# An output projection as seven block products instead of eight, in a one-core hybrid encoder layer

## The chip, the cores and the metric

The kernel runs on one core of a Trainium2 chip. The metric is the device time of one execution in microseconds. A profiled execution also gives a span, from its first to its last instruction. The engines are TensorE (PE in the profile), VectorE (DVE), ScalarE (ACT), GpSimd (POOL) and SyncE (SP), whose queue issues the transfers here.

## The reference

Sequence length and model width are 1024, one layer. Everything is float32.

```python
h = layer_norm(x, emb_ln_g, emb_ln_b)
proj = h @ w_in                      # q k v z_a u z_b g_a g_b
y_a = neighbourhood_attention(q, k, v, rpb) * silu(z_a)      # 8 heads x 64
u = centred_depthwise_conv(u, conv_w, conv_b)
y_b = (rg_lru(u, forward) + rg_lru(u, backward)) * silu(z_b)
m = sigmoid(g_a + b_merge[0]) * (y_a @ w_ba) + sigmoid(g_b + b_merge[1]) * (y_b @ w_bb)
out = m @ w_out
return layer_norm(ALPHA * h + out, ln_g, ln_b)
```

The change concerns the last three lines: the merged branches `m` (1024 tokens by 1024 channels), the product `m @ w_out` with a 1024 by 1024 weight, and the closing layer norm.

## The kernel before

**Products in three passes.** An operand is split into a high part, its cast to the matmul's fp32r type, and a low part, the remainder (`lo_of`, line 127: a subtraction on VectorE or GpSimd). `mm3` (line 130) multiplies high by high, low by high and high by low, so each block of 128 rows of the contraction costs three matmuls.

**The stages.** A first layer norm, the input projection, the convolution and the recurrences, then the second branch's product together with the attention, then the first branch's product with the merge, then the output projection. VectorE, ScalarE, GpSimd and SyncE follow the order in which the code is written (`manual_schedule`), and so does TensorE: each engine's queue is in order, and an instruction that waits holds up what is behind it on its engine. Across engines only data and buffers order the work.

**The input projection** already uses seven block products instead of eight (`OPS`, line 145; s1 to s4 are sums of weight blocks, T1 to T4 sums of the activations). This scheme is Winograd's form of Strassen's product for a 2 by 2 split of both operands: four sums on each operand, seven products, and sums of the results.

**The branch slots** (line 1316): 16 slots, two for each of the eight channel blocks `j`, one for each half `n` of the tokens. In a slot TensorE makes `mb`, twelve matmuls of 512 columns, in a PSUM bank. VectorE multiplies by the gate (`b_gate`, line 1013) and adds the second branch's part `m` (`merge`, line 1300), ScalarE casts to the high part `mh`, VectorE subtracts for the low part `ml`. Beside that ScalarE and GpSimd split the next branch weight (`b_split`) and one row block of the output weight, `wo`, 128 by 1024, in two slots.

**The output projection** (line 1390): for each of eight token tiles `i` two halves of 512 columns (the last tile's second half in two pieces of 256), each 24 matmuls into one bank (`o_product`). VectorE adds the scaled residual `z` (loaded from `h_d`) and takes statistics. Then `newton` makes the reciprocal root, ScalarE scales the row, GpSimd multiplies by the gain and adds the bias (`gb2`), SyncE stores it. The last tile is finished by VectorE alone, in four pieces. Banks are taken in turn from the tags mb, s and tp, two banks each; the banks of `acc` stay unused here.

Of the kernel before, what the change touches and what calls it, by code (L numbers as in the profile page):

```python
# [10 lines left out]
F32 = mybir.dt.float32  # L11
F32R = mybir.dt.float32r
# [55 lines left out]
def encoder_kernel(ctx, tc, x, gb1, gb, w_qk, w_v, w_s, w_ba, w_bb, w_gate, smalls, bias, w_out, out):  # L68
# [58 lines left out]
    def lo_of(eng, lo, full, hi):  # L127
        eng.tensor_tensor(lo, full, hi.bitcast(F32), ALU.subtract)  # L128
# [10 lines left out]
    def run(gen):  # L139
        for _ in gen:  # L140
            pass
# [865 lines left out]

    def b_group(which, j, n, y, o, ks=range(4)):

        yield from mm3(o[:], [([t[:, k, :] for t in b_w[which, j]], [t[:, k, halves[n]] for t in y]) for k in ks],  # L1010
                       quantum=1, first=ks[0] == 0, last=ks[-1] == 3)

    def b_gate(which, j, n, o):
# [61 lines left out]

    yb = late["yb"]
    yap = pool("yap")
    ya = pair(yap, [P, 4, S], "ya")
    at0 = pool("at0")
    acc = [pst.tile([P, HALF], F32, name=f"acc{g}") for g in range(2)]  # L1080
# [103 lines left out]

    def gated(h, n):
        hp = h // 2
        at_, (hi, lo) = attns[hp][:, halves[n]], [t[:, hp, halves[n]] for t in ya]
        G.tensor_tensor(at_, at_, gates[hp][:, halves[n]], ALU.mult)
        G.tensor_copy(hi, at_)
        lo_of(G, lo, at_, hi)  # L1190

    def last_half(g):

        h, hp = H - 1, H // 2 - 1

        def product(n):
            at_ = attns[hp][:, halves[n]]
            V.tensor_tensor(at_, at_, gates[hp][:, halves[n]], ALU.mult)
            A.copy(ya[0][:, hp, halves[n]], at_)

        def low(n):
            lo_of(V, ya[1][:, hp, halves[n]], attns[hp][:, halves[n]], ya[0][:, hp, halves[n]])
# [23 lines left out]
    for unit in range(-NT, H * NT + PV_LAG):  # L1226
# [50 lines left out]
        if unit == H * NT:  # L1277

            for pl in (late["hd"], late["hd0"], late["ybp"]):
                pl.release()  # L1280
            wop = pool("wop", "right")
            wo = [pair(wop, [P, D], f"wo{k}") for k in range(NK - 2)]
            wos = {}

            def w_load(k):
                if k < NK:
                    wos[k] = wop.tile([P, D], F32, tag="wos", bufs=3, name=f"wos{k}")
                    SP.dma_start(wos[k][:], w_out[k * P:(k + 1) * P, :])
# [4 lines left out]
            for k in range(3):  # L1293
                w_load(k)
    assert filled == sum(FILL)


    sums_m, mh, ml = {}, {}, {}

    def merge(j, n, o):  # L1300
        b_gate(0, j, n, o)
        V.tensor_tensor(o[:], o[:], late["m", j, n][:], ALU.add)
        mh[j, n] = late["mp"].tile([P, HALF], F32R, tag=f"m{j}{n}", name=f"mh{j}{n}")
        A.copy(mh[j, n][:], o[:])

    def merge_lo(j, n, o):
        lo_of(V, ml[j, n][:], o[:], mh[j, n][:])
# [6 lines left out]
    banks[0] = pst  # L1314
    turns.append(itertools.chain(["mb", "mb", "s"], itertools.cycle(["tp", "mb", "s"])))
    for slot in range(2 * NK + 2):
        j, n = divmod(slot, 2)
        if 2 < slot <= 2 * NK:
            merge(*divmod(slot - 1, 2), sums_m[slot - 1])
        if slot == 2:  # L1320
            at0.release()
            mlp = pool("mlp")
            ml.update({(j, n): mlp.tile([P, HALF], F32R, name=f"ml{j}{n}") for j in range(NK) for n in range(2)})
            wo += [pair(mlp, [P, D], f"wo{k}") for k in range(NK - 2, NK)]
            merge_lo(0, 0, sums_m.pop(0))
        for q in (1,) if slot == 3 else (slot - 2,) if slot > 3 else ():
            merge_lo(*divmod(q, 2), sums_m.pop(q))
        if j < NK:
            if n == 0:
                b_load(0, j + 2)  # L1330
            g_load(0, j + 1, n, **(dict(tag=f"u{slot % 4}", bufs=1) if slot % 4 else dict(tag="z", bufs=5)))
            o = sums_m[slot] = bank(f"mb{j}{n}")

            run(b_group(0, j, n, ya, o, range(3 if slot < 2 else 4)))
            if 0 < slot < 3:
                run(b_group(0, 0, slot - 1, ya, sums_m[slot - 1], range(3, 4)))
            if n == 0 and j > 0:
                b_split(0, j + 1, A)
            if 0 < slot < 3:
                merge(0, slot - 1, sums_m[slot - 1])  # L1340

        if slot % 2:
            if j < NK:
                A.copy(wo[j][0][:], wos[j][:])
            if j > 0:
                w_load(j + 2)
        elif slot > 0:
            lo_of(G, wo[j - 1][1][:], wos.pop(j - 1)[:], wo[j - 1][0][:])
        if slot == 9:
            zp = pool("zp")  # L1350
            gb2 = zp.tile([P, 2, D], F32, name="gb2")
            zs = {}

            def load_z(i):
                if i < NT:
                    zs[i] = zp.tile([P, D], F32, tag="z", bufs=4, name=f"z{i}")
                    SP.dma_start(zs[i][:], h_d[i])

        elif slot in (10, 12, 14):
            load_z(slot // 2 - 5)  # L1360
        elif slot in (11, 13):
            SP.dma_start(gb2[:, :, halves[slot // 13]], gb[slot // 13])


    def o_product(i, cols):
        o = bank(f"o{i}_{cols.start}")
        w = cols.stop - cols.start
        run(mm3(o[:, :w], [([t[k, i // 4][:, ti(i)] for t in (mh, ml)], [t[:, cols] for t in wo[k]])
                           for k in range(NK)]))
        return o[:, :w]  # L1370

    def small(name, n, bufs=2):
        return zp.tile([P, n], F32, tag=name[:2], bufs=bufs, name=name)

    def newton(mv, i, other):

        sd, ve = small(f"sd{i}", 1), small(f"ve{i}", 3)
        A.activation(sd[:], mv[:, 1:2], AF.Sqrt, bias=eps_z[:])  # L1378
        V.tensor_scalar(ve[:, 0:1], mv[:, 1:2], EPS * TWICE * TWICE, -0.5, ALU.add, ALU.mult)
        next(other, None)  # L1380
# [6 lines left out]
            pass  # L1387
        return sd, ve

    for i in range(NT):  # L1390
        last = i == NT - 1
        load_z(i + 3)
        z = zs.pop(i)
        piece = 256 if last else HALF
        pieces = [slice(c, c + piece) for c in range(0, D, piece)]
        st = small(f"{'ls' if last else 'st'}{i}", 6 * len(pieces))
        for cols in [halves[0]] + (pieces[2:] if last else [halves[1]]):
            o = o_product(i, cols)
            V.scalar_tensor_tensor(z[:, cols], z[:, cols], ALPHA * TWICE, o, ALU.mult, ALU.add)  # L1399
            for c, part in enumerate(pieces):  # L1400
                if cols.start <= part.start < cols.stop:
                    V.bn_stats(st[:, 6 * c:6 * c + 6], z[:, part])
        mv = small(f"mv{i}", 2)
        V.bn_aggr(mv[:], st[:].rearrange("p (c s) -> p c s", s=6))  # L1404
        if not last:
            sd, ve = newton(mv, i, iter(()))
            V.tensor_scalar(ve[:, 2:3], mv[:, 0:1], -1.0, sd[:], ALU.mult, ALU.mult)
            A.activation(z[:], z[:], AF.Identity, bias=ve[:, 2:3], scale=sd[:])  # L1408
            G.tensor_tensor(z[:], z[:], gb2[:, 0, :], ALU.mult)  # L1409
# [4 lines left out]
        def scaled():  # L1414
            for part in pieces:
                V.scalar_tensor_tensor(z[:, part], z[:, part], mv[:, 0:1], gb2[:, 0, part], ALU.subtract, ALU.mult)
                yield

        sd, ve = newton(mv, i, scaled())
        for part in pieces:  # L1420
            V.scalar_tensor_tensor(z[:, part], z[:, part], sd[:], gb2[:, 1, part], ALU.mult, ALU.add)
            SP.dma_start(out[i][:, part], z[:, part])
    order.__exit__(None, None, None)
    for pl in (zp, mlp, yap, late["mp"], cst, wop, late["wb"], ev, dram, banks[0]):
        pl.release()


# [81 lines left out]
```

## Time and profile before

| | |
|---|---|
| median of 3 runs | 676.06 us (675.43 to 676.21) |
| profiled execution | 676.07 us |
| its span | 674.3 us |
| granted TensorE clock, mean | 0.998 |
| busy, share of the span: PE, DVE, ACT, POOL | 98%, 74%, 54%, 53% |
| 600 to 620 us: busy DVE, ACT, POOL of 20.00 us | 7.98, 3.08, 8.86 us |

A row of a timeline gives the start in us, the length in us, the engine, the line of the code, the operation, the written and the read tiles with their shapes, and the count where equal instructions in a row are merged; in brackets stands the idle time ahead and what ended it. Consecutive instructions of an engine overlap a little, so the distance of two starts is what one costs in a full queue. A row of groups gives busy time in us and the mean in ns after the bar. In the chain that ended last each row is a stretch of one engine's work that released the next.

### The profile page before, as it was taken

What the parts mean: (1) busy time and instruction counts of PE and PEld (TensorE: products, weight loads), DVE (VectorE), ACT (ScalarE), POOL (GpSimd) and SP (SyncE); (2) the same over time, 40 slices, a digit from 0 to 9 for tenths busy, and PEclk for the clock granted to TensorE, in tenths of its full rate; (3) what the DMA queues carried; (4) which work ended last, traced back from release to release, by engine and by line L of the source; (5) the groups of instructions that cost most, each with busy time, mean ns of one, the idle gap of its engine ahead of it and who ended that gap; (6) DMA issues with size and microseconds to landing.
All of it is one profiled execution on the core that took longest, in us unless ns stands there. A gap on an engine that the chain in (4) does not pass through costs nothing.

```text
span 674.3 us, 9352 instructions
## 1 busy us (share of the span) xinstructions
PE 663.7 (98%) x3189; PEld 554.3 (82%) x3189; DVE 498.9 (74%) x835; ACT 364.5 (54%) x615; POOL 354.4 (53%) x261
## 2 busy tenths in 40 slices
PE   8999999999999999999999999999999999999995
PEld 7888888888888887888788888888888888888884
DVE  6978876985998699879968785477788787443334
ACT  6555433357786676669576634477777555210110
POOL 5898263433676575567647544115255456334432
PEclk9999999999999999999999999999999999999999
DMA  8746616033344033531543557998794467412211
GB/s 322 246 152 228 209 41 221 36 125 109 126 143 150 22 108 110 172 126 48 202 172 124 172 186 261 339 332 308 251 317 146 163 232 280 170 62 94 93 63 62
DMA packets 48990, 113.40 MB, mean 168 GB/s; under 512 B 5088, under 2 KB 9776, under 8 KB 47408
## 3 DMA queue, kind: packets, MB, share of 16 engines
q1 hardware_dynamic: 48912, 112.81, 48.0%
q8 instruction: 25, 0.41, 0.2%
q14 instruction: 21, 0.17, 0.1%
q10 hardware_dynamic: 32, 0.01, 0.0%
HBM read 77.11 MB, written 35.68 MB: 167 GB/s over the span
## 4 chain that ended last, share of the span: by engine, by line
PE 76%; DVE 9%; issue 4%; POOL 1%; ACT 1%; DMA 1%; SPq 0%; DVEq 0%; POOLq 0%
PE a L134 28%; PE o L134 13%; PE mb L134 13%; PE s L134 11%; PE acc L1145 4%; PE s L1099 3%; PE pt L1121 3%; PE g L794 2%; POOL ht_l L128 1%; DVE ws_l L128 1%; DVE wa_l L128 1%; DMA a_2f<-in_w_s_dram 1%; DVE uc L752 1%; ACT ht_h L312 1%; DVE s_12f L384 0%
## 5 line engine op out<-in xcount | busy, mean ns | idle before, releaser
L134 PE MATMUL a<-ht_h,ws_h 128*128 128x512 f32 x136 | 53.1, 391 | 0.0
L134 PE MATMUL a<-ht_h,ws_l 128*128 128x512 f32 x136 | 53.0, 389 | 0.0
L134 PE MATMUL a<-b_h,wa_l 128*128 128x512 f32 x136 | 53.0, 389 | 0.0
L134 PE MATMUL a<-ht_l,ws_h 128*128 128x512 f32 x136 | 52.9, 389 | 0.0
L134 PE MATMUL a<-b_h,wa_h 128*128 128x512 f32 x136 | 52.9, 389 | 0.0
L134 PE MATMUL a<-b_l,wa_h 128*128 128x512 f32 x136 | 52.9, 389 | 0.0
L134 PE MATMUL o<-wo_h,ml 128*128 128x512 f32 (+1 forms) x136 | 51.2, 377 | 0.0
L134 PE MATMUL o<-wo_l,mh 128*128 128x512 f32 (+1 forms) x136 | 51.2, 376 | 0.0
L134 PE MATMUL o<-wo_h,mh 128*128 128x512 f32 (+1 forms) x136 | 51.2, 376 | 0.0
L1109 DVE CUSTOM_DVE_ANT_0 sc<-s,bias 128x384 f32<-128x384 f32 (+1 forms) x64 | 33.3, 522 | 21.5 <-PE s L1099 14.1
L1399 DVE SCALAR_TENSOR_TENSOR z<-z,o 128x512 f32<-128x512 f32 (+1 forms) x17 | 11.2, 656 | 51.1 <-PE o L134 51.1
L1129 ACT CAST pt_h<-pt 128x384 fp32r<-128x384 f32 x64 | 29.0, 453 | 25.3 <-PE pt L1121 17.3
L1409 POOL TENSOR_TENSOR z<-z,gb 128x1024 f32<-128x1024 f32 x7 | 16.8, 2397 | 48.6 <-ACT z L1408 48.6
L1114 ACT ACTIVATE p<-sc,summ 128x384 f32<-128x384 f32 (+1 forms) x64 | 37.8, 591 | 5.5 <-DVE summ L1109 5.3
L1378 ACT ACTIVATE sd<-mv,eps_z 128x1 f32<-128x1 f32 x8 | 2.4, 294 | 67.1 <-DVE mv L1404 67.1
L128 DVE TENSOR_TENSOR pt_l<-pt,pt_h 128x384 fp32r<-128x384 f32 x64 | 33.2, 519 | 2.1 <-ACT pt_h L1129 1.6
L326 PE MATMUL v<-wv,b_h 128*128 128x512 f32 x128 | 32.8, 398 | 0.2 <-ACT b_h L279 0.2
L902 POOL CAST wb_h<-wb 128x512 fp32r<-128x512 f32 x9 | 7.0, 778 | 49.3 <-DMA wb<-in_w_bb_dram 49.3
L128 POOL TENSOR_TENSOR ht_l<-t,ht_h 128x512 fp32r<-128x512 f32 x16 | 22.0, 1408 | 19.9 <-ACT ht_h L312 19.9
L1099 PE MATMUL s<-ks,qs 128*128 128x384 f32 (+1 forms) x128 | 31.5, 327 | 0.0
L134 PEld LDWEIGHTS a<-ht_h,ws_h 128*128 128x128 f32 x136 | 25.5, 188 | 5.9 <-issue 0.4
L1121 PEld LDWEIGHTS pt<-ident,p 128*128 128x128 f32 x176 | 23.1, 140 | 8.5
(455 smaller groups left out, 2192.4 us busy)
## 6 DMA issues: line engine op xcount, KB each, us to landing
ks<-k_d SPq DMA_DIRECT2D x8, 1024.0 KB, 8.3
h_d<-x SPq DMA_DIRECT2D x8, 512.0 KB, 5.0
v_d<-vs SPq DMA_DIRECT2D x8, 512.0 KB, 3.5
q_d<-q SPq DMA_DIRECT2D x8, 512.0 KB, 3.0
ga_d<-ga SPq DMA_DIRECT2D x16, 256.0 KB, 2.2
gb_d<-gb SPq DMA_DIRECT2D x16, 256.0 KB, 2.4
k_d<-k SPq DMA_DIRECT2D x8, 512.0 KB, 3.4
qs<-q_d SPq DMA_DIRECT2D x8, 512.0 KB, 5.2
```

Source lines behind the costliest of these rows:

```text
L128: eng.tensor_tensor(lo, full, hi.bitcast(F32), ALU.subtract)
L134: PE.matmul(o, a, b, start=first and i == 0, stop=last and i == len(prods) - 1, skip_group_check=not (first and last))
L326: PE.matmul(vos[i][:], a, wv[kind == "w"][k][:], start=vn[i] == 0, stop=vn[i] == 23)
L794: PE.matmul(o[:, n, :], w[:, 2 * d + b, :], us[b][:, n * HALF:(n + 1) * HALF], start=z == 0, stop=z == 1)
L1099: PE.matmul(o[:, :P * len(near(t))], q[:, t * P:(t + 1) * P], k[:, z, keys], start=z == 0, stop=z == 1)
L1109: V.tensor_tensor_reduce(s[:, :w], o[:, :w], heads[h][2][:, b0:b0 + w], -1.0, 3.0e38, ALU.add, ALU.min, accum_out=sums[h][0][:, t:t + 1])
L1114: A.activation(probs[h % 2][t][:], scs.pop((h, t))[:, :w], AF.Exp, bias=sums[h][0][:, t:t + 1], scale=-1.0, accum_out=sums[h][1][:, t:t + 1])
L1121: PE.transpose(tp[:, n * P:(n + 1) * P], probs[h % 2][t][:, z * P:(z + 1) * P], ident[:])
L1129: A.copy(pt[0][:, span(b)], tps[h, b][:, :P * len(near(b))])
L1145: PE.matmul(acc[g][:, d:d + w], vvs[h // 2][:, b, h % 2, :], pt[:, a:a + w], start=b in (1, 6) and z == 0, stop=z == 1 and b == (4, 7)[g])
L1399: V.scalar_tensor_tensor(z[:, cols], z[:, cols], ALPHA * TWICE, o, ALU.mult, ALU.add)
L1409: G.tensor_tensor(z[:], z[:], gb2[:, 0, :], ALU.mult)
```

## The change

The output projection becomes seven block products. Both halves of the tokens (rows 0 to 511 and 512 to 1023, four tiles `p` each) and both halves of the channels of `m` and of the columns of `w_out` are the blocks a11 to a22 and b11 to b22; `c` counts the four 128-row blocks of the contraction within a half. With s1 = a21 + a22, s2 = s1 - a11, s3 = a11 - a21, s4 = a12 - s2, and t1 = b12 - b11, t2 = b22 - t1, t3 = b22 - b12, t4 = b21 - t2, TensorE makes 28 products of twelve matmuls (`PLAN`, `LAST`): a11 b11, a12 b21, s2 t2, s1 t1, s4 b22, s3 t3, a22 t4, for p = 0 to 3. They are gathered in two sets of four banks: X (a11 b11, then s2 t2, s3 t3 and a22 t4 on top of it) and W (a12 b21; later s1 t1 and s4 b22 on top). VectorE reads a bank between the products that are added to it. Rows of tokens p and p + 4 belong together: row p is finished after s4 b22, row p + 4 after a22 t4.

Other parts: every branch slot begins with the split of the next branch weight (`b_split` ahead of the slot's other work; before, it came after the slot's matmuls); a list `jobs` says in which slot each sum, cast and low part stands; t1 and the raw s3 are made on GpSimd (eight sums), the other sums on VectorE; the low parts of w_out's blocks, of t1 to t4 and of s1 on GpSimd; banks come from a fixed ring of eight; `ya` is split into one tile for each block and half; w_out, z and the gains move in pieces of 128 by 512; GpSimd's gain and bias work on 512 columns; the last row is held in PSUM banks until it is scaled.

```diff
-    for slot in range(2 * NK + 2):
...
+    RING = ("mb", "mb", "s", "tp", "acc0", "s", "tp", "acc1")
...
+    def split_lo(slot):
...
+        if j < 4 and n:
+            t = raw["s3", c] = place(("s3", c), ap, f"s3l{c}", F32)
+            minus(t[:], late["m", c, 0][:], late["m", c, 1][:], G)
+            return
...
+    def second(c, o):
+        V.tensor_tensor(late["m", c, 1][:], late["m", c, 1][:], o[:], ALU.add)
+        minus(o[:], late["m", c, 1][:], late["m", c, 0][:])
+        high("s2", c, o[:], late["mp"], f"m{c}0")
+
+    def fourth(c, o):
+        low("s2", c, o[:], ap, f"s2l{c}")
+        minus(o[:], late["m", c + 4, 0][:], o[:])
+        high("s4", c, o[:], late["mp"], f"m{c + 4}0")
...
+        if slot > 1:
+            jobs.setdefault(slot + 1, [])[:0] = [lambda s=slot: merge(s), lambda s=slot: split(s)]
+        job(slot + 2, split_lo, slot)
+        if n and j >= 4:
+            job(slot + 2, lambda c, s: second(c, got[s]), j - 4, slot)
+            job(slot + 3, lambda c, s: fourth(c, got[s]), j - 4, slot)
+            job(slot + 4, lambda c, s: fourth_lo(c, got[s]), j - 4, slot)
...
+        job(2 * c + 3, t1, c)
...
+        job(17 + c, t2, c)
+        job(17 + c, t4, c)
+        job(17 + c, lambda c: w_high("t2", c, yap, f"y1{c}0"), c)
+        job(18 + c, lambda c: w_low("t2", c, raw["t2", c], yap, f"y0{c}1"), c)
...
+    def finished(p, r):
+        mv = mean_var(p, r)
+        sd, ve = newton(mv, f"{p}{r}", iter(()))
+        V.tensor_scalar(ve[:, 2:3], mv[:, 0:1], -1.0, sd[:], ALU.mult, ALU.mult)
+        for n in range(2):
+            z = zs[p, r, n]
             A.activation(z[:], z[:], AF.Identity, bias=ve[:, 2:3], scale=sd[:])
-            G.tensor_tensor(z[:], z[:], gb2[:, 0, :], ALU.mult)
-            G.tensor_tensor(z[:], z[:], gb2[:, 1, :], ALU.add)
-            SP.dma_start(out[i], z[:])
+            G.tensor_tensor(z[:], z[:], gbs[0, n][:], ALU.mult)
+            G.tensor_tensor(z[:], z[:], gbs[1, n][:], ALU.add)
+            SP.dma_start(out[p + 4 * r][:, halves[n]], z[:])
...
+    LAST = [("s3", "t3", 0), ("s3", "t3", 1), ("a22", "t4", 0), ("s3", "t3", 2), ("a22", "t4", 1), ("s3", "t3", 3),
+            ("a22", "t4", 2), ("a22", "t4", 3)]
+    PLAN = [("a11", "b11", range(4)), ("a12", "b21", range(4)), ("s2", "t2", range(4)), ("s1", "t1", (0, 1)),
+            ("s4", "b22", (0, 1)), ("s1", "t1", (2, 3)), ("s4", "b22", (2, 3))]
...
+        jobs.setdefault(17 + n, []).insert(0, lambda a=a, p=p: EVAC[a](p))
```

Here is VectorE's queue where the branch slots end, before. L1020 is the gate, L1302 the merge, L128 a low part:

```order
L1020 SCALAR_TENSOR_TENSOR mb70_5970<-g070_5921,mb70_5970 128x512
L1302 TENSOR_TENSOR mb70_5970<-mb70_5970,m170_5454 128x512
L128 TENSOR_TENSOR ml61_5649<-mb61_5950,mh61_5967 128x512
L1020 SCALAR_TENSOR_TENSOR mb71_5991<-g071_5948,mb71_5991 128x512
L1302 TENSOR_TENSOR mb71_5991<-mb71_5991,m171_5578 128x512
L128 TENSOR_TENSOR ml70_5650<-mb70_5970,mh70_5988 128x512
```

The same place after the change, from the merge of the last branch slot on. L1354 and L1324 are sums, L1497 reads bank X of row 0 into z; m131 becomes s1, mb71 then holds s2, wb22 and wb21 are raw blocks of w_out:

```order
L1331 TENSOR_TENSOR mb71_6035<-mb71_6035,m171_5582 128x512
L128 TENSOR_TENSOR s2l2_6055<-mb61_5981,s2h2_6031 128x512
L1324 TENSOR_TENSOR mb61_5981<-m160_5260,mb61_5981 128x512
L128 TENSOR_TENSOR a12l3_6060<-mb70_6007,a12h3_6022 128x512
L1497 SCALAR_TENSOR_TENSOR z000_6064<-z000_6064,x0_6072 128x512
L128 TENSOR_TENSOR s4l2_6086<-mb61_5981,s4h2_6058 128x512
L128 TENSOR_TENSOR a22l3_6088<-mb71_6035,a22h3_6053 128x512
L1354 TENSOR_TENSOR m131_4718<-m131_4718,mb71_6035 128x512
L1324 TENSOR_TENSOR mb71_6035<-m131_4718,m130_4602 128x512
L1324 TENSOR_TENSOR t20_6096<-wb22_0_5708,t10_5683 128x512
L1324 TENSOR_TENSOR wb21_0_5822<-wb21_0_5822,t20_6096 128x512
```

Where each branch slot gave VectorE three instructions, the sums for s1, s2 and s4, their low parts and then the weight sums t2 and t4 now stand between the merges and behind them.

GpSimd's queue at the end of the weight splits, before (wo_l is a low part of 1024 columns, z0 the first finished row):

```order
L128 TENSOR_TENSOR wb07_l_5937<-wb07_5868,wb07_h_5932 128x512
L128 TENSOR_TENSOR wo5_l_5563<-wos5_5807,wo5_h_5562 128x1024
L128 TENSOR_TENSOR wo6_l_5653<-wos6_5857,wo6_h_5652 128x1024
L128 TENSOR_TENSOR wo7_l_5655<-wos7_5913,wo7_h_5654 128x1024
L1409 TENSOR_TENSOR z0_5890<-z0_5890,gb2_5862 128x1024
```

After the change, from the last branch weight on; t2l, s1l, t1l are low parts:

```order
L128 TENSOR_TENSOR wb07_l_5933<-wb07_5885,wb07_h_5932 128x512
L128 TENSOR_TENSOR b21l0_6062<-wb21_0_5822,b21h0_5947 128x512
L128 TENSOR_TENSOR b21l1_6066<-wb21_1_5850,b21h1_5977 128x512
L128 TENSOR_TENSOR b21l2_6068<-wb21_2_5881,b21h2_6005 128x512
L128 TENSOR_TENSOR b21l3_6070<-wb21_3_5913,b21h3_6033 128x512
L128 TENSOR_TENSOR t2l0_6128<-t20_6096,t2h0_6099 128x512
L128 TENSOR_TENSOR t2l1_6157<-t21_6132,t2h1_6135 128x512
L128 TENSOR_TENSOR s1l0_6182<-m101_4069,s1h0_6130 128x512
L128 TENSOR_TENSOR t2l2_6186<-t22_6161,t2h2_6164 128x512
```

Behind these rows stand the rest of 24 low parts in all from t2l0 on, and 28 instructions for the gain and bias of seven rows, one low part (t4l3) among them.

SyncE's last issues, before and then after:

```order
L1411 DMA out_0_dram<-z5_6154 128x1024
L1411 DMA out_0_dram<-z6_6225 128x1024
L1422 DMA out_0_dram<-z7_6296 128x256 x4
```

```order
L1494 DMA out_0_dram<-z110_6441 128x512
L1494 DMA out_0_dram<-z111_6345 128x512
L1494 DMA out_0_dram<-z210_6477 128x512
L1494 DMA out_0_dram<-z211_6372 128x512
L1598 DMA out_0_dram<-z310_6513 128x256 x2
L1598 DMA out_0_dram<-z311_6401 128x256 x2
```

The four pieces of the last row stand last in both; ahead of them stands the row before it, in the changed kernel in two halves; that row's last product is TensorE's last but one.

More of the change, by code (lines that the diff above doesn't have):

```diff
@@ L1281, in encoder_kernel, with w_load @@
             wop = pool("wop", "right")
[L1282 to L1288, printed above, removed]
+            raw = {}
+            def w_load(o, c):
+                k, n = ("b11", "b12", "b21", "b22").index(o) // 2 * 4 + c, int(o[2]) - 1
+                t = raw[o, c] = wop.tile([P, HALF], F32, tag=f"{o}{c}", name=f"w{o}_{c}")
+                SP.dma_start(t[:], w_out[k * P:(k + 1) * P, halves[n]])
             b_load(0, 1)
@@ new lines, in high, with low, minus, merge @@
+    def high(o, c, src, pl, tag, **kw):
+        t = hi[o, c] = place((o, "h", c), pl, tag, **kw)
+        A.copy(t[:], src)
+    def low(o, c, src, pl, tag, eng=V):
+        t = lo[o, c] = place((o, "l", c), pl, tag)
+        lo_of(eng, t[:], src, hi[o, c][:])
+    def minus(out_, a, b, eng=V):
+        eng.tensor_tensor(out_, a, b, ALU.subtract)
+    def merge(slot):
+        j, n = divmod(slot, 2)
+        c, o, m = j % 4, got[slot], late["m", j, n]
+        b_gate(0, j, n, o)
+        dst = m if j < 4 and n else o
+        V.tensor_tensor(dst[:], o[:], m[:], ALU.add)
@@ L1313, in encoder_kernel @@
     assert not todo
-    banks[0] = pst
-    turns.append(itertools.chain(["mb", "mb", "s"], itertools.cycle(["tp", "mb", "s"])))
-    for slot in range(2 * NK + 2):
+    for slot in range(16):
         j, n = divmod(slot, 2)
[L1318 to L1362, printed above, removed]
@@ new lines, in encoder_kernel, with scaled @@
+    assert not jobs, sorted(jobs)
+    p, x, w = 3, banksX[3], banksW[3]
+    for c, part in enumerate((slice(0, 256), slice(256, HALF))):
+        o = ring(c, f"y{c}")
+        o_product("a22", "t4", p, o[:, :256], part)
+        V.tensor_tensor(w[:, part], zs[p, 1, 0][:, part], o[:, :256], ALU.add)
+        V.bn_stats(stats[p, 1][:, 6 * c:6 * c + 6], w[:, part])
+    pieces = [(n, slice(a, a + 256)) for n in range(2) for a in (0, 256)]
+    mv = mean_var(p, 1)
+    def scaled():
+        for n, part in pieces:
+            o = (w, x)[n][:, part]
+            V.scalar_tensor_tensor(o, o, mv[:, 0:1], gbs[0, n][:, part], ALU.subtract, ALU.mult)
+            yield
@@ L1423, in encoder_kernel @@
+    sd, ve = newton(mv, "last", scaled())
+    for n, part in pieces:
+        z = zs[p, 1, n]
+        V.scalar_tensor_tensor(z[:, part], (w, x)[n][:, part], sd[:], gbs[1, n][:, part], ALU.mult, ALU.add)
+        SP.dma_start(out[p + 4][:, halves[n]][:, part], z[:, part])
     order.__exit__(None, None, None)
-    for pl in (zp, mlp, yap, late["mp"], cst, wop, late["wb"], ev, dram, banks[0]):
+    for pl in (zp, ap, yap, late["mp"], cst, wop, late["wb"], ev, dram, pst):
         pl.release()
```

223 lines of the change are left out of this document (172 added, 51 removed).

## The prediction

> **What bounds the kernel now.** I read the first part of the page, then the chain that ended last, then the timelines of the tail. The page:
>
> ```profile
> span 674.3 us, 9352 instructions
> PE 663.7 (98%) x3189; PEld 554.3 (82%) x3189; DVE 498.9 (74%) x835; ACT 364.5 (54%) x615; POOL 354.4 (53%) x261
> ```
>
> The profiled execution took 676.07 us, 1.77 more than its span. The median of the three runs is 676.06, so sums made in the span and raised by 1.77 can be compared with the runs directly. The chain (start, length, engine and tile, count):
>
> ```profile
> 400.33 2.72 PE s L134 x12
> ...
> 535.19 43.59 PE mb L134 x192
> 578.77 87.36 PE o L134 x408
> 670.26 0.79 DVE z L1421 x2
> ```
>
> From 535.19 to 666.13 the chain is TensorE without a gap; it is the bound, and twelve 512-wide matmuls cost 2.72 us. I call that a slot: slots 0 to 15 are the branch sums, slot 16 starts at 578.77, slot k at 578.77 + 2.72 (k - 16). VectorE's timeline shows the last two output pieces and the end:
>
> ```profile
> 654.97 0.69 DVE L1399 SCALAR_TENSOR_TENSOR z<-z,o 128x512 f32<-128x512 f32 x1 [3.96 <-PE o L134]
> ...
> 657.81 0.21 DVE L1407 TENSOR_SCALAR ve<-mv,sd 128x1 f32<-128x1 f32 x1
> ...
> 663.29 0.42 DVE L1399 SCALAR_TENSOR_TENSOR z<-z,o 128x256 f32<-128x256 f32 x1 [1.34 <-PE o L134]
> 663.74 0.43 DVE L1402 BATCH_NORM_STATS2 ls<-z 128x6 f32<-128x256 f32 x1
> ...
> 666.16 0.42 DVE L1399 SCALAR_TENSOR_TENSOR z<-z,o 128x256 f32<-128x256 f32 x1 [1.99 <-PE o L134]
> ...
> 667.08 0.26 DVE L1404 BATCH_NORM_AGGREGATE mv<-ls 128x2 f32<-128x24 f32 x1
> ```
>
> 24 matmuls of 256 columns take 666.16 - 663.29 = 2.87 us. One row's closing on VectorE, from its last piece to ve, takes 658.02 - 654.97 = 3.05. From the aggregate to the end of the span are 674.3 - 667.08 = 7.22 us.
>
> **TensorE: -11.06 us.** Before, the output projection is 360 matmuls of 512 and 48 of 256. After, it is 28 products of twelve: 27 at 2.72 and the last as two halves of 1.43, 76.30 us against 87.36. Unhindered, TensorE ends at 655.07 instead of 666.13. The rest of the sum is who cannot follow that. Per token row the work on the other engines stays in kind; what is added is four sums and their splits on each operand, and the additions of partial products.
>
> **VectorE's queue, slots 10 to 20.** Its rate where it works without waiting:
>
> ```profile
> 543.21 0.69 DVE L128 TENSOR_TENSOR ml<-mb,mh 128x512 fp32r<-128x512 f32 x1 [0.66 <-ACT mh L1304]
> ...
> 550.33 0.68 DVE L128 TENSOR_TENSOR ml<-mb,mh 128x512 fp32r<-128x512 f32 x1
> ```
>
> These starts are eleven instructions apart in 7.12 us, 0.647 each, so a slot holds 4.2. Before, a slot brings three. After, the order gives slots 10 to 16 3, 5, 5, 6, 5, 6 and 5: from slot 11 on an excess of 0.8, 0.8, 1.8, 0.8, 1.8, 0.8, together 6.8 instructions or 4.4 us at the start of slot 17 (581.49). There t20, the first weight sum, stands sixth: 3.9 us more, it ends near 589.8, three slots late. That costs TensorE nothing yet. The latest bank wanted back is that of slot 15, for slot 23 at 597.8; its last reader, s4l3, stands eight instructions behind t20, near 595. But t20 is wanted by ScalarE (t2h0), then GpSimd (t2l0), and GpSimd's queue is in order: it stands still until then. A cast takes about 0.6 (rows below), so GpSimd starts t2l0 at 590.5.
>
> **GpSimd from 590.5: the term that decides.**
>
> ```profile
> 548.53 0.59 ACT L1304 CAST mh<-mb 128x512 fp32r<-128x512 f32 x1 [0.39 <-DVE mb L1302]
> 549.01 0.62 ACT L900 CAST wb_h<-wb 128x512 fp32r<-128x512 f32 x1
> 520.75 1.30 POOL L1188 TENSOR_TENSOR attn<-attn,za 128x512 f32<-128x512 f32 x1 [0.50 <-DVE attn L1156]
> 522.12 0.61 POOL L1189 CAST ya_h<-attn 128x512 fp32r<-128x512 f32 x1
> 522.81 1.29 POOL L128 TENSOR_TENSOR ya_l<-attn,ya_h 128x512 fp32r<-128x512 f32 x1
> 524.05 0.60 POOL L902 CAST wb_h<-wb 128x512 fp32r<-128x512 f32 x1
> ```
>
> A 512-wide GpSimd TENSOR_TENSOR costs 1.24 to the next independent start, 1.37 where the next needs its result. From t2l0 the order has 24 low parts, 24 x 1.24 = 29.8, and for each of seven rows two multiplications and two additions, 2 x (1.37 + 1.24) = 5.22, 36.5 in all. One gap I add: t21 stands five instructions behind t20 (3.2 us), its cast behind two others, while t2l0 lasts 1.24; t2l1 starts 2.3 us late. That is 68.6 us and reaches 659.1, if nothing else touches GpSimd. But:
>
> ```profile
> 534.43 2.56 POOL L1183 TENSOR_TENSOR za<-za,rsb 128x512 f32<-128x512 f32 x2 [8.40 <-DMA rsb<-rs_d]
> 536.93 1.76 POOL L128 TENSOR_TENSOR wb_l<-wb,wb_h 128x512 fp32r<-128x512 f32 x1
> 535.92 1.61 DVE L1198 TENSOR_TENSOR attn<-attn,za 128x512 f32<-128x512 f32 x1
> ...
> 538.27 0.96 DVE L128 TENSOR_TENSOR ya_l<-attn,ya_h 128x512 fp32r<-128x512 f32 x1
> 539.16 0.68 DVE L1198 TENSOR_TENSOR attn<-attn,za 128x512 f32<-128x512 f32 x1
> ...
> 659.43 2.39 POOL L1409 TENSOR_TENSOR z<-z,gb 128x1024 f32<-128x1024 f32 x1 [6.01 <-ACT z L1408]
> 660.47 0.69 DVE L1399 SCALAR_TENSOR_TENSOR z<-z,o 128x512 f32<-128x512 f32 x1 [2.44 <-PE o L134]
> ```
>
> The same VectorE product takes 0.68 alone and 1.61 when it comes while GpSimd is inside an instruction: it ends 0.6 after GpSimd's second one does, and GpSimd's third takes 1.76 instead of 1.29. Both its inputs lie in SBUF. The row at 660.47 has one input in PSUM and loses nothing, nor does GpSimd. [...]
>
> Of such VectorE instructions twelve fall after t2l1 has begun: t2 and t4 of the third and fourth blocks, four t3, four low parts of s3. They cost GpSimd between nothing (the 659.43 row) and 12 x 0.6 = 7.2; I take 7.2, since the three meetings at 535 to 539 are the like ones. GpSimd then ends at 590.5 + 68.6 + 7.2 = 666.3. They cost VectorE up to 1.24 + 0.6 each.
>
> **TensorE's waits.** With GpSimd late, slot 24 (600.53) just gets t2l3: four low parts and two of s1, the gap and four meetings from 590.5 end near 602.7, and the last of the twelve matmuls, which reads it, starts at 603.0. t1l3, eight low parts and four meetings on, ends near 615.0 and is wanted in slot 28 at 613.9: a wait of 1.1. In slot 30 TensorE adds onto a bank that VectorE must have read (z011); VectorE, held at t3 and s3, gets there about 2.0 later than TensorE. So 0 to 3.1 us of waits; with 3.1 TensorE ends at 658.2. All lower parts after that are in time.
>
> **The tail.** Two ends run side by side. VectorE closes row 2 in 3.05 while the last product takes 2.86, then does two pieces of 0.45 + 0.45, then the 7.22: 658.2 + 0.2 + 1.8 + 7.2 = 667.4. GpSimd's end gates SyncE:
>
> ```profile
> 534.18 1.46 SPq L1288 DMA_DIRECT2D wos<-in_w_out_dram  x3
> ...
> 669.89 1.79 SPq L1422 DMA_DIRECT2D out_dram<-z  x4
> ```
>
> After GpSimd's last addition SyncE issues that half row and only then the four pieces of the last row, which stand behind it: five issues at 0.43 to 0.49, 2.2 us. Before, the last issue ended at 671.68 and the span 2.62 later. 666.3 + 2.2 + 2.6 = 671.1, later than 667.4. With 1.77: **673.0 us**, 3 less than before. Of the 11.06 freed, 8 are lost to GpSimd starting late, being held up, and holding SyncE.
>
> Moves at no cost: the weight split ahead of each slot's other work (its cast and low part have two slots, and GpSimd's extra sums in slots 3 to 11 bring a pair of slots to four instructions, 5.0 of 5.44 us); without that cover a branch slot waits about 1.3. The copies on ScalarE: at most four per slot at 0.5 to 0.6, 2.4 of 2.72. The loads of w_out are the same bytes in smaller pieces.
>
> **Rivals.**
> *The meetings are cheap.* For it: VectorE has slack after slot 21 and could fall between GpSimd's instructions. Then the low parts end at 590.5 + 29.8 + 2.3 = 622.6; row 0 can be scaled only after slot 30 (619.6) plus 3.05 and a 0.6 activation, 623.4; t4l3 and the 36.5 follow, 661.1; plus 2.2 + 2.6, 665.9, against 664.3 for TensorE and VectorE. **667.7 us.** Against it: 1.76 against 1.29. Chance 0.20.
>
> *VectorE's queue is slower than 0.647, and the change loses.* The rate is from a stretch where each row read PSUM and none waited long. The grouped rows of the input stage hold a slower one:
>
> ```profile
> L847 DVE TENSOR_TENSOR zs<-w,zs 128x512 f32<-128x512 f32 x8 | 6.9, 865 | 0.1
> ```
>
> Here splits wait for casts that wait for sums on the same queue. At 0.80 a slot holds 3.4, the excess at slot 17 is 11.6 instructions or 9.3 us, t20 ends at 581.49 + 9.3 + 4.8 = 595.6, 5.8 later, and everything on GpSimd with it: **678.8 us**. It decides from about 0.76 (4.4 us later) on; between 0.70 and 0.76 the result is no change. Against: in slots 11 to 16 GpSimd is nearly idle, so meetings are few. Chances 0.17 slower, 0.13 no change.
>
> *TensorE's waits are longer.* It moves nothing up to 3.7 us more, since GpSimd's end is later; the two ends then meet.
>
> **How the numbers follow.** My forecast has 0.50: 673.0. The range takes in the cheap meetings and most of the slow queue, 667 to 678.5. Faster by over 0.2% (about what a measurement of this kernel tells from no change, 1.35 us) is the forecast and the first rival, 0.70; same 0.13; slower 0.17.
>
> **What would show it.** TensorE's output rows: 348 instead of 408, ending near 658. VectorE: t20 ending near 590. GpSimd: idle before t2l0, then solid to about 666, with low parts of 1.8 among those of 1.29; VectorE's t3 rows near 1.8 instead of 0.68. SyncE: the last row's pieces issued after GpSimd's last addition, not after VectorE. Wrong would be: gaps of TensorE inside slots 0 to 23, GpSimd done before VectorE's last row, or t20 later than 594.

## The result: slower by 0.6%, and the profile after

The changed kernel takes 680.18 us in the median of six runs (678.79 to 681.32), the kernel before 676.12 (675.43 to 676.53) beside it. The ratio is 1.0059, with a 95% interval of 1.0046 to 1.0072. The forecast was 673.0, faster; the measured time lies on the other side of no change and outside the range. The profiled execution of the changed kernel took 680.35 us, 4.28 more than that of before, although TensorE has 60 matmuls fewer.

The head of its page (the spans of before were 674.3 and 663.7 busy on TensorE):

```profile
span 678.5 us, 9458 instructions
PE 655.1 (97%) x3129; PEld 545.6 (80%) x3129; DVE 529.7 (78%) x880; ACT 385.1 (57%) x662; POOL 390.6 (58%) x307
```

Up to 614 us the trace goes nearly as forecast. In the timelines of VectorE and GpSimd (start, length, then what ran and, in brackets, the idle time ahead and its releaser) the first weight sum t20 ends at 589.15 (forecast: near 590), and GpSimd stands idle before t2l0 and again before t2l1:

```profile
585.94 0.68 DVE L128 TENSOR_TENSOR s4l<-mb,s4h 128x512 fp32r<-128x512 f32 x1
586.54 0.68 DVE L128 TENSOR_TENSOR a22l<-mb,a22h 128x512 fp32r<-128x512 f32 x1
...
588.46 0.69 DVE L1324 TENSOR_TENSOR t<-wb,t 128x512 f32<-128x512 f32 x1
...
590.00 1.30 POOL L128 TENSOR_TENSOR t2l<-t,t2h 128x512 fp32r<-128x512 f32 x1 [5.18 <-ACT t2h L1317]
593.59 1.29 POOL L128 TENSOR_TENSOR t2l<-t,t2h 128x512 fp32r<-128x512 f32 x1 [2.29 <-ACT t2h L1317]
```

Then the chain that ended last (start, length, engine and tile; rows of under 0.5 us are left out) is no longer TensorE's alone, as it was from 535 us on before. GpSimd and VectorE hand work to each other, TensorE comes in only at 625.74, and GpSimd closes:

```profile
618.35 1.27 POOL t3l L128
619.65 0.70 DVE s3l L128
620.42 1.26 POOL b22l L128
...
623.10 1.27 POOL t3l L128
625.01 0.69 DVE z L1497
625.74 19.20 PE w L134 x72
...
664.02 0.70 DVE z L1497
...
668.34 1.28 POOL z L1492
...
```

From 664.02 on these are the steps that finish row 6, on VectorE, ScalarE and GpSimd. GpSimd, busy without a gap since 635.19, waited only 0.40 for that row: TensorE's path and GpSimd's queue reach the end almost together.

The same stretch in the timelines of VectorE, GpSimd and TensorE shows who waited for whom:

```profile
616.21 0.69 DVE L128 TENSOR_TENSOR s3l<-s,s3h 128x512 fp32r<-128x512 f32 x1 [6.80 <-POOL t3l L128]
619.65 0.69 DVE L128 TENSOR_TENSOR s3l<-s,s3h 128x512 fp32r<-128x512 f32 x1 [2.15 <-POOL t3l L128]
624.40 0.69 DVE L128 TENSOR_TENSOR s3l<-s,s3h 128x512 fp32r<-128x512 f32 x1 [3.46 <-POOL t3l L128]
625.01 0.68 DVE L1497 SCALAR_TENSOR_TENSOR z<-z,w 128x512 f32<-128x512 f32 x1
...
616.98 1.29 POOL L128 TENSOR_TENSOR b22l<-wb,b22h 128x512 fp32r<-128x512 f32 x1 [0.81 <-DVE s3l L128]
635.19 1.29 POOL L1492 TENSOR_TENSOR z<-z,gb 128x512 f32<-128x512 f32 x1 [5.30 <-ACT z L1491]
...
625.74 0.79 PE L134 MATMUL w<-b22h,s4h 128*128 128x512 f32 x1 [7.64 <-DVE z L1497]
```

VectorE's low parts of s3 wait for GpSimd's low parts of t3, although neither computes anything from the other. GpSimd's b22l and t4l wait for VectorE's s3l in turn, four times 0.81. Three of the s3l stand on VectorE ahead of z011 (the row at 625.01: it reads bank W of p = 0 into row 4), which frees the bank that TensorE wants in slot 30: TensorE waits 7.64 us. And GpSimd, out of work at 629.9, waits 5.30 for the first row.

The cause is a line of the code. Low parts made by `w_low` get their place from a chain: each is written where the whole block lay from which the previous one has just been taken.

```python
def w_low(o, c, full, *home, eng=G):
    homes[o, c] = spare.pop()
    spare.append(home)
    low(o, c, full[:], *homes[o, c], eng)
```

The chain follows the order of the code: t3l0, s3l0, b22l2, t3l1, s3l1, b22l3 and so on. All are GpSimd's but s3l (`eng=V`). So s3l0 is written where the raw t3 lay, and may start when t3l0 has read it; b22l2 is written where the raw s3 lay, and may start when s3l0 has read it. Two queues in order are tied to each other by places alone.

The wait also cost clock. Busy time of PE, PEld, DVE, ACT and POOL, then the granted TensorE clock, DMA share and GB/s, by stretch:

```profile
620.00:621.00 1.00, 0.00 (x0) 0.00 (x0) 0.94 (x2) 0.00 (x0) 0.58 (x1) 1.00 0.00 0
622.00:623.00 1.00, 0.00 (x0) 0.00 (x0) 0.00 (x0) 0.00 (x0) 1.00 (x1) 0.50 0.00 0
626.00:630.00 4.00, 4.00 (x10) 3.13 (x11) 1.29 (x2) 0.00 (x0) 3.00 (x3) 0.50 0.02 4
```

After the wait twelve matmuls start 0.427 apart instead of 0.227, and the 72 matmuls of the chain's row take 19.20 us where six slots of 2.72 are 16.3: 2.9 us. SyncE issues the last row's pieces behind GpSimd, as forecast, only later:

```profile
672.25 1.27 POOL L1493 TENSOR_TENSOR z<-z,gb 128x512 f32<-128x512 f32 x1
...
673.97 1.88 SPq L1598 DMA_DIRECT2D out_dram<-z  x4
```

### The profile page after: what moved, and what is told of

It is laid out like the page before. It is cut to its first block, busy times and chain, and to the rows that moved or that the text cites. A ratio compares the mean times of both kernels' runs of the same rounds, so it can differ in the third digit from the quotient of the medians.

```text
span 678.5 us, 9458 instructions
## 1 busy us (share of the span) xinstructions
PE 655.1 (97%) x3129; PEld 545.6 (80%) x3129; DVE 529.7 (78%) x880; ACT 385.1 (57%) x662; POOL 390.6 (58%) x307
## 5 line engine op out<-in xcount | busy, mean ns | idle before, releaser
L134 PE MATMUL mb<-ya,wb_h 128*128 128x512 f32 x128 | 39.6, 389 | 0.0
L128 DVE TENSOR_TENSOR pt_l<-pt,pt_h 128x384 fp32r<-128x384 f32 x64 | 33.2, 519 | 2.1 <-ACT pt_h L1131 1.6
L128 POOL TENSOR_TENSOR ht_l<-t,ht_h 128x512 fp32r<-128x512 f32 x16 | 22.0, 1410 | 20.0 <-ACT ht_h L312 20.0
L134 PEld LDWEIGHTS a<-ht_l,ws_h 128*128 128x128 f32 x136 | 25.5, 188 | 5.4
L134 PEld LDWEIGHTS a<-b_h,wa_h 128*128 128x128 f32 x136 | 25.5, 188 | 5.4
L134 PEld LDWEIGHTS a<-b_h,wa_l 128*128 128x128 f32 x136 | 25.5, 188 | 5.4
L134 PEld LDWEIGHTS a<-b_l,wa_h 128*128 128x128 f32 x136 | 25.5, 188 | 5.3
L134 PEld LDWEIGHTS a<-ht_h,ws_l 128*128 128x128 f32 x136 | 25.5, 188 | 5.3
```

Of the source, the lines that this page charges most:

```text
L134: PE.matmul(o, a, b, start=first and i == 0, stop=last and i == len(prods) - 1, skip_group_check=not (first and last))
```

## The experiments

The kernel before took 675.51 to 675.86 us beside them, in the median of its runs. Ratios are to it. Differences to the changed kernel are taken from its 680.18, which was measured beside a before of 676.12; by the ratios they come out 0.3 to 0.8 smaller.

**The low parts of s3 in places of their own.** One line, on the changed kernel; the new places are tiles of `ya` that are free by then.

```diff
-        job(26 + c, lambda c: w_low("s3", c, raw["s3", c], ap, f"s3l{c}", eng=V), c)
+        job(26 + c, lambda c: low("s3", c, raw["s3", c][:], yap, f"y1{c}1"), c)
```

> The low parts of s3 get places of their own (tiles that TensorE has finished with by slot 24) and leave the chain of handed-on places; no instruction moves on any queue. Buffer theory: in the changed kernel VectorE waited 14.6 us in four low parts of s3 for GpSimd's low parts of t3, whose source places they were to be written into, and z011, which TensorE needs for slot 30, stood behind three of them. Without it the 7.6 us wait of TensorE falls to under 2, its clock stays at full rate, GpSimd starts row 0 near 629 instead of 635.2, and the time is 673 to 675 us, about 6 less. Lock theory (meetings of VectorE and GpSimd in SBUF are what delays z011): the wait of slot 30 stays above 5 us and the time above 678.

Measured: 672.92 us, ratio 0.9956 [0.9941, 0.9971]; 7.3 less than the changed kernel, and faster than before. In its timelines GpSimd has no gap from t2l1 to its end. The wait of slot 30 is gone; TensorE's one wait left is 2.06, in slot 28, and against the expectation the clock did fall once behind it (last section):

```profile
628.39 1.30 POOL L1492 TENSOR_TENSOR z<-z,gb 128x512 f32<-128x512 f32 x1
...
664.97 1.26 POOL L1493 TENSOR_TENSOR z<-z,gb 128x512 f32<-128x512 f32 x1
...
615.88 0.50 PE L134 MATMUL w<-t1l,s1h 128*128 128x512 f32 x1 [2.06 <-POOL t1l L128]
```

The gains begin at 628.39 instead of 635.19 and GpSimd ends at 666.23, where the forecast had put it (666.3). The span is 671.2, the time 0.1 from the 673.0 of the forecast: without the tie the forecast's chain of steps is the one that runs. That the number fits so closely is in part luck (two sizes make up for each other, see what held, below).

**The low parts of s3 in the chain, but on GpSimd.** This keeps the chain of places and takes away only that it crosses from one queue to another.

```diff
-        job(26 + c, lambda c: w_low("s3", c, raw["s3", c], ap, f"s3l{c}", eng=V), c)
+        job(26 + c, lambda c: w_low("s3", c, raw["s3", c], ap, f"s3l{c}"), c)
```

> The changed kernel with the four low parts of s3 left in the chain of handed-on places, but made by GpSimd instead of VectorE, so that no place passes from one engine's queue to another's. If it is the handing over between two queues in order that costs the time, TensorE's wait ahead of slot 30 and GpSimd's four waits of 0.8 go, and GpSimd has four low parts of 1.3 to 1.4 more than with places of their own, where it was done at 666.23: done near 671.6, 678 to 678.6 in all. If the chain of places itself is what stalls, whoever fills it, the wait ahead of slot 30 stays and the time is 681 to 685.

Measured: 676.82 us, ratio 1.0018 [1.0009, 1.0027]. The wait for VectorE is gone; TensorE now waits 2.42 in slot 30 for b22l3, which stands behind s3l in GpSimd's queue. GpSimd is done at 669.46, 3.2 later than with own places, where 5.4 were expected: t2l0 started 0.76 earlier in this run (589.18), and without VectorE's s3l its low parts from 608 to 631 take 1.26 to 1.30, while with own places four of those from 609 to 618 take 1.60 to 1.71. TensorE's wait and GpSimd's last addition in the timelines:

```profile
622.22 0.50 PE L134 MATMUL w<-b22l,s4h 128*128 128x512 f32 x1 [2.42 <-POOL b22l L128]
...
668.20 1.26 POOL L1493 TENSOR_TENSOR z<-z,gb 128x512 f32<-128x512 f32 x1
```

Taken with the run before, in which VectorE kept its s3l and waited for none of them: the chain of places within one queue leaves GpSimd without a gap, handing places from one queue in order to another stalled both in the changed kernel (GpSimd four times 0.81 us, VectorE up to 6.80). Whether moving z011 ahead of the s3l would have been enough was not tried. The expectation for this run had missed that the meetings of s3l go as well.

**The clock held.** 32 matmuls of zeros onto bank X of row 0, ahead of slot 30. The output is unchanged by them.

```diff
+        if slot == 30:
+            for _ in range(32):
+                PE.matmul(banksX[0][:], hold[:], held[:], start=False, stop=False, skip_group_check=True)
```

> Adds 32 matmuls of zeros (512 columns) in the wait ahead of slot 30, onto a bank that VectorE has read; they change no value. In the changed kernel the first thirteen matmuls after the 7.6 us wait start 0.427 us apart instead of 0.227. If that is the price of the idle time, the clock stays at full rate, these matmuls are back at 0.227, row 0 and all behind it come 2.5 us earlier: 677.5 to 678. If the slow rate has another cause, nothing changes: 680.

Measured: 678.32 us, ratio 1.0038 [1.0023, 1.0053]: 1.9 us less than the changed kernel. In TensorE's timeline the zeros fill the wait, and the matmuls behind it take 0.39 again:

```profile
617.51 7.08 PE L1580 MATMUL x<-held,hold 128*128 128x512 bf16 x32
625.33 0.50 PE L134 MATMUL w<-b22h,s4h 128*128 128x512 f32 x1 [0.74 <-DVE z L1497]
625.66 0.39 PE L134 MATMUL w<-b22h,s4l 128*128 128x512 f32 x1
```

The bank still comes free only at 625.3. So of the 7.3 us that the tie costs, up to 1.9 are the clock (1.4 by the ratios; t2l0 also started 0.43 earlier in this run), and the rest is the wait. It is less than the 2.5 expected; TensorE, now faster, waits another 0.44 for VectorE one slot later.

**Without the four t3 sums.** The raw b12 stands in for t3, so the output differs; VectorE loses four instructions with two SBUF inputs.

```diff
-        t = raw["t3", c] = raw["b12", c]
-        minus(t[:], raw["b22", c][:], t[:])
+        raw["t3", c] = raw["b12", c]
```

> Leaves out the four sums t3 (the product s3 t3 then uses b12), that is four VectorE instructions with two SBUF inputs that fall among GpSimd's low parts; the chain of places stays. Lock: GpSimd's low parts between 601.8 and 609 go from 1.84 to about 1.3 us, t3l of block 0 starts 2 us earlier (612.7), and z011 and the time follow by 2 us: 678. If the meetings cost GpSimd nothing, its rows stay and the time is 680. Buffer theory says nothing else: TensorE still waits 5 to 6 us ahead of slot 30.

Measured: 677.31 us, ratio 1.0022 [1.0013, 1.0031]: 2.9 less. GpSimd's four low parts beside them fall from 1.84 to 1.30. The first of them in this run's timeline:

```profile
601.02 1.30 POOL L128 TENSOR_TENSOR t1l<-t,t1h 128x512 fp32r<-128x512 f32 x1
```

and in the changed kernel's:

```profile
601.78 1.84 POOL L128 TENSOR_TENSOR t1l<-t,t1h 128x512 fp32r<-128x512 f32 x1
```

Four times 0.54 is 2.2, and t2l0 started 0.76 earlier in this run (589.24). A meeting with a t3 sum costs GpSimd nearly what the forecast took (0.6). TensorE still waits 6.96 ahead of slot 30, more than the 5 to 6 expected: the meetings are not what holds z011.

**The t2 sums first.** In VectorE's lists of slots 17 to 20, t2 moves to the front.

```diff
-        job(17 + c, t2, c)
...
+    for c in range(4):
+        jobs[17 + c].insert(0, lambda c=c: t2(c))
```

> The sums t2 of the four blocks stand first in VectorE's list of slots 17 to 20 instead of fifth or later. If t20 gates GpSimd's chain from t2l on (my step), t20 ends 3 us earlier, t2l of block 0 starts near 587, and the chain of low parts, z011 and the end come up to 3 us earlier: 677 to 678.5, less if the later t2 gate. If the chain is set only by the handed-on places further on, the time stays at 680.

Measured: 679.71 us, ratio 1.0061 [1.0044, 1.0077], not to be told from the changed kernel. The sum came 3.3 earlier, and GpSimd's t2l0 did not. The timelines of VectorE, ScalarE and GpSimd:

```profile
585.17 0.68 DVE L1324 TENSOR_TENSOR t<-wb,t 128x512 f32<-128x512 f32 x1
...
589.06 0.59 ACT L1317 CAST s2h<-mb 128x512 fp32r<-128x512 f32 x1 [3.73 <-DVE mb L1324]
589.54 0.62 ACT L1317 CAST t2h<-t 128x512 fp32r<-128x512 f32 x1
...
590.30 1.29 POOL L128 TENSOR_TENSOR t2l<-t,t2h 128x512 fp32r<-128x512 f32 x1 [5.66 <-DVE t L1324]
```

t20's cast t2h0 stands on ScalarE behind the cast of s2's last block, and that one waits 3.73 for its sum from VectorE. So t20 alone does not set GpSimd's start, as the prediction had it; VectorE's queue does, but through s2 as well. What an earlier t2l0 would bring, this run leaves open.

**Two parts of the change undone.** First the eight sums (t1 and the raw s3) on VectorE instead of GpSimd; then the branch weight's split behind the slot's other work, as before.

```diff
-            minus(t[:], late["m", c, 0][:], late["m", c, 1][:], G)
+            minus(t[:], late["m", c, 0][:], late["m", c, 1][:])
...
-        minus(t[:], raw["b12", c][:], raw["b11", c][:], G)
+        minus(t[:], raw["b12", c][:], raw["b11", c][:])
```

> The changed kernel with its eight sums (t1 and the raw s3) on VectorE instead of GpSimd. They stand in slots 3 to 9, where VectorE has three to four instructions a slot and room for 4.2. If that room is real, nothing moves: 679.5 to 680.8, as the changed kernel. If VectorE's queue is already full there, up to eight instructions of 0.647 more stand ahead of t20, 5.2 us, and the time is up to 685.

```diff
-        if slot < 16 and n == 0 and j > 0:
-            b_split(0, j + 1, A)
         for f in jobs.pop(slot, ()):
             f()
...
+            if n == 0 and j > 0:
+                b_split(0, j + 1, A)
             continue
```

> The changed kernel with the branch weight's split behind the other work of its slot, as it was before the change. If the split has two slots of cover either way, nothing moves: 679.5 to 680.8. If the split first in the slot is what keeps the branch slots without a gap, each of the six slot pairs from the second on waits about 1.3, up to 8 us: 688.

Measured: 679.69 us (ratio 1.0056 [1.0042, 1.0070]) and 679.76 us (1.0059 [1.0045, 1.0074]). Neither part moves the time here. In the second, the waits of TensorE show one in the branch slots (us in total, times, longest):

```profile
PE mb L134 <- POOL wb_l L128: 0.8, 1, 0.8
```

In the first, t2l0 starts no later than with the sums on GpSimd, so VectorE did have that room in slots 3 to 9; its GpSimd timeline:

```profile
589.12 1.30 POOL L128 TENSOR_TENSOR t2l<-t,t2h 128x512 fp32r<-128x512 f32 x1 [5.17 <-ACT t2h L1317]
```

**What bounds the kernel once the tie is gone.** Three more runs, each with s3's low parts in places of their own. In the first the splits of s1 move up into GpSimd's idle time before t2l0 (ScalarE's casts with them):

```diff
-        job(18 + c, lambda c: high("s1", c, late["m", c, 1][:], yap, f"y0{c}0"), c)
...
-        job(20 + c, lambda c: w_low("s1", c, late["m", c, 1], late["mp"], f"m{c}1"), c)
...
+    for o, c, at in (("b21", 0, 16), ("b21", 1, 16), ("b21", 2, 16), ("s1", 0, 16), ("s1", 1, 16), ("b21", 3, 16),
+                     ("s1", 2, 16)):
...
+    jobs[15][:0] = [lambda c=c: high("s1", c, late["m", c, 1][:], yap, f"y0{c}0") for c in (0, 1)]
...
+    jobs[18].append(lambda: w_low("s1", 3, late["m", 3, 1], late["mp"], "m31"))
```

> The low parts of s3 in places of their own, and besides that the splits of s1 moved up on ScalarE and GpSimd: s1l0 to s1l2 beside b21l3 (580 to 587, where GpSimd stood idle), s1l3 between t2l0 and t2l1. If GpSimd's queue from t2l0 to its last addition now sets the end, with SyncE's five issues behind it, the 19 low parts that are left before row 0 (about 1.5 each with meetings) end near 620, row 0 can be scaled from 623.4, t4l3 and 28 gains and biases follow: GpSimd ends near 661 and the time is 667.5 to 668.5. If TensorE and VectorE's closing of the last rows set the end as well (VectorE was done at 665.35 with s1 late), only SyncE's queue behind GpSimd is won, 1 to 2 us: 671 to 672. If neither bounds it, no change from 672.9.

Measured: 669.44 us, ratio 0.9906 [0.9892, 0.9920]. In its timeline GpSimd does low parts of s1 from 580.68 on and is done at 662.69:

```profile
580.68 3.00 POOL L128 TENSOR_TENSOR s1l<-m,s1h 128x512 fp32r<-128x512 f32 x2
...
661.43 1.26 POOL L1501 TENSOR_TENSOR z<-z,gb 128x512 f32<-128x512 f32 x1
```

It is 3.5 us below own places alone, just what GpSimd's end moved (666.23 to 662.69), and SyncE's last pieces go out behind that end in both. That GpSimd's queue alone bounded that kernel the run does not show: TensorE waits nowhere any more in the last 90 us, and VectorE's end moved 4.1 with it (665.35 to 661.23). The time is 0.9 above the upper end expected; GpSimd now waits 1.34 to 1.40 before each further low part of t2, since VectorE makes these sums no faster.

In the second SyncE issues the two halves of row 6 behind the last row's four pieces instead of ahead of them (own places, s1 late); in the third both edits are together.

```diff
-            SP.dma_start(out[p + 4 * r][:, halves[n]], z[:])
+            if (p, r) != (2, 1):
+                SP.dma_start(out[p + 4 * r][:, halves[n]], z[:])
...
+    for n in range(2):
+        SP.dma_start(out[6][:, halves[n]], zs[2, 1, n][:])
```

> The low parts of s3 in places of their own, and SyncE issues the two halves of row 6 behind the last row's four pieces, not ahead of them. If SyncE's queue behind GpSimd's last addition sets the end, the four pieces go out as VectorE makes them (the last written at 665.35) and two issues follow GpSimd: three issues of 0.45 less, 1 to 1.4 us, 671.6 to 671.9 against 672.9. If the halves of 512 columns, now last, take longer to land than the pieces of 256, some of it is given back: 672.3 to 673.

> The splits of s1 early, the low parts of s3 in places of their own, and row 6's halves issued behind the last row's four pieces. With s1 early GpSimd is done at 662.69 and VectorE at 661.23. If the four issues of the last row behind GpSimd's last addition set the end, SyncE issues them from about 661.6 and the two halves behind 663: three issues less, 668.0 to 668.4 against 669.4. If what is left is the time the last bytes take to land, wherever the issues stand: 669.2 to 669.6.

Measured: 671.06 us (ratio 0.9932 [0.9917, 0.9946]), 1.9 less than 672.92; and 667.27 us (0.9879 [0.9862, 0.9895]), 2.2 less than 669.44. Both are more than the 1 to 1.4 expected. SyncE's last issues with late s1:

```profile
662.65 1.81 SPq L1599 DMA_DIRECT2D out_dram<-z  x4
664.55 1.78 SPq L1601 DMA_DIRECT2D out_dram<-z  x2
```

and with both edits, where GpSimd's last addition is shown too:

```profile
659.32 1.80 SPq L1607 DMA_DIRECT2D out_dram<-z  x4
661.21 1.07 SPq L1609 DMA_DIRECT2D out_dram<-z  x2
...
660.67 1.26 POOL L1501 TENSOR_TENSOR z<-z,gb 128x512 f32<-128x512 f32 x1
```

From GpSimd's end (661.93) to the end of the span (665.1) are 3.2 us, against 5.0 with the old order of issues; with late s1 it is 3.2 as well. So the order is worth 1.8: only about 0.35 of issuing is left behind GpSimd's end, not the two issues expected. The rest, in the profiled executions, is that GpSimd itself ended earlier, 0.3 with late s1 and 0.8 with early s1; the new order does not explain that. The last kernel beats both: 8.2 us below before, 12.2 to 12.9 below the changed kernel. Of the 11.06 that the seven products free on TensorE it keeps three quarters.

## Why the prediction was wrong

**The step that failed: TensorE's wait in slot 30.** The prediction said that VectorE, "held at t3 and s3", gets to z011 about 2.0 us later than TensorE. Measured: 7.64, and 2.9 more for the slow clock behind it. How the 2.0 is added up the prediction does not show; the s3 low parts stand in it only with their meetings with GpSimd, up to 1.24 + 0.6 each. That their place is that of t3's raw block, so that three of them wait for the 15th, 17th and 20th low part of GpSimd's queue, is missing; the order of instructions does not show it, the line `homes[o, c] = spare.pop()` does. The prediction's own terms would have given the wait: through t3l2 stand 20 low parts, a gap and ten meetings, 590.5 + 2.3 + 20 x 1.24 + 10 x 0.6 = 623.6; s3l2 and z011 behind it end near 624.9, against TensorE's 617.95. The trace has z011 from 625.01 to 625.69.

**The bound that failed with it: "it moves nothing up to 3.7 us more".** TensorE came to its first matmul of slot 30 at 625.74 instead of 619.95, 5.8 later, and lost 2.9 to the clock: 658.2 + 8.7 = 666.9, the end of its last matmul in the trace. That is past the 3.7. But GpSimd was not just overtaken: row 0 is finished from slot 30's bank, so GpSimd's gains and biases began at 635.19, not at the 628.5 of the forecast's terms (590.5 + 2.3 + 23 x 1.24 + 7.2). The wait entered both ends. GpSimd ended at 673.52 instead of 666.3, the span 4.98 after it (forecast: 4.8).

**What held.** The seven products themselves: no gap in the branch slots and none in slots 16 to 27. VectorE's queue: t20 at 589.15 against 589.8. t2l1 2.29 late against 2.3. TensorE's wait in slot 28: 1.14 against 1.1. The tail: SyncE's last issues behind GpSimd. The 24 low parts and the 28 gains take, in the run with own places, nearly what was forecast: 589.94 to 666.23 is 76.3 against 75.8. In that sum two sizes are off and make up for each other: a low part costs 1.37 to the next start, not 1.24 (each waits for the one before it, whose place it takes), 3.1 us more for 24; and the meetings came to 4.9, not 7.2 (the means over 1290 ns in its groups of GpSimd instructions, four each: busy us, mean ns, idle before):

```profile
L128 POOL TENSOR_TENSOR s1l<-m,s1h 128x512 fp32r<-128x512 f32 x4 | 6.9, 1733 | 0.3
L128 POOL TENSOR_TENSOR t1l<-t,t1h 128x512 fp32r<-128x512 f32 x4 | 6.6, 1638 | 0.3
L128 POOL TENSOR_TENSOR b22l<-wb,b22h 128x512 fp32r<-128x512 f32 x4 | 6.2, 1552 | 0.3
L128 POOL TENSOR_TENSOR t2l<-t,t2h 128x512 fp32r<-128x512 f32 x4 | 5.9, 1465 | 7.6 <-ACT t2h L1317 7.5
```

One sign of the forecast was wrong within this: VectorE's t3 rows were to show 1.8 and show 0.68; there GpSimd alone pays, 1.84 instead of 1.30. The prices of a meeting in the forecast, 12 x 0.6 for GpSimd and up to 1.24 + 0.6 for VectorE, were the author's estimate from the rows at 535 to 539 of before; no run shows them for all twelve sums and low parts. In the changed kernel the two t2 take 1.20 and 1.18, the two t4 1.61 each, t3 and s3l 0.68 to 0.69 (the s3l while GpSimd waits), and the low parts on GpSimd take 1.62 to 1.64 beside t2 and t4 and 1.83 to 1.85 beside t3. The first of the t3 rows in VectorE's timeline of the changed kernel, beside GpSimd's row at 601.78:

```profile
601.79 0.68 DVE L1324 TENSOR_TENSOR wb<-wb,wb 128x512 f32<-128x512 f32 x1
```

**The rivals.** The slower one, 678.8, named the right sign and nearly the time, but by a mechanism that did not run, so its number is luck: VectorE's queue went at 0.63 per instruction (four from 585.94 to 588.46 above), a little faster than the 0.647 taken, and t20 was early. Cheap meetings are ruled out by the rows of 1.84 and by the run without t3. That the cover of the weight splits matters was not borne out: undone, it cost one wait of 0.8 that reached nothing. Two sums of the prediction are 0.1 off: 671.1 and 1.77 make 672.9, and in the first rival 619.6, 3.05 and 0.6 make 623.3.

## What to carry to other kernels

When two engines with queues in order share a pool of places, the order in which places are handed on is a dependency like any other: list for each instruction that is moved between engines not only what it reads, but what must have been read before its place is free, and where that stands in the other queue. An instruction that frees a bank TensorE wants should not stand behind such a hand-over (argued from the trace; no run moved it). When a change frees time on the bound engine, price the engine that becomes the bound from its first late start to its last instruction, and what is issued behind it: here one line about places was worth 7.3 us, four splits moved into an idle stretch 3.5 (TensorE's last wait went with them), and the order of the last six transfers 1.8.

## What the runs showed of the hardware that was not expected

The granted TensorE clock fell after waits much shorter than the 7.64 us above, and there once work had resumed. From TensorE's timeline with own places:

```profile
617.37 0.57 PE L134 MATMUL w<-t1l,s1h 128*128 128x512 f32 x1
617.74 0.63 PE L134 MATMUL w<-t1h,s1h 128*128 128x512 f32 x1
...
620.73 0.45 PE L134 MATMUL w<-b22h,s4l 128*128 128x512 f32 x1
621.01 0.39 PE L134 MATMUL w<-b22l,s4h 128*128 128x512 f32 x1
```

Here TensorE waited 2.06 us and resumed at 615.88; from 617.4 to 620.8 it ran slower, eight matmuls 0.2 longer each (0.63 against 0.39 in the rows above), 1.6 us lost. With s3's low parts on GpSimd it waited 2.42, resumed at 622.22, and from 623.1 to 626.5 its matmuls took up to 0.63 as well (granted clock 0.94 over 626 to 630, 1.00 over 632 to 634). Both slow stretches last 3.4 us. Behind the 7.64 of the changed kernel the granted clock is 0.50 from 621.1 to 631.3, 10.2 us. The wait of 1.14 in the changed kernel had no slow stretch behind it (granted clock 1.00 from 614 to 621), nor did that of 1.15 with s3's low parts on GpSimd (0.39 a matmul again until the wait of 2.42). Nor had one of the same 2.06, in the run with own places and row 6 issued last (late s1); the mean granted clock of that execution was 0.995, with own places alone 0.99:

```profile
615.60 0.50 PE L134 MATMUL w<-t1l,s1h 128*128 128x512 f32 x1 [2.06 <-POOL t1l L128]
```

So 2.06 was followed by a slow stretch in one execution and by none in the other. What decides between them these runs do not show.
